# Recurrent gates of a hybrid decoder layer: a block's high and low halves stacked on the contraction

## The chip, the cores and the metric

The kernel runs on one core of one Trainium2 chip. The metric is the device time of one execution in microseconds (us). The core has a matrix engine (TensorE, PE in the profile), a vector engine (VectorE, DVE), an activation engine (ScalarE, ACT), GpSimd (POOL) and a queue that issues transfers (SyncE, SP). Each engine takes its instructions strictly in the order of its own queue; they meet only through semaphores.

## The reference, cut to what matters

One decoder layer on 512 tokens of width 1024, in fp32. A combined projection gives the inputs of a recurrent branch (`u_x`, `u_g`), of an attention branch (`q`, `k`, `v`) and two branch gates. The part that is changed is the two gates of the recurrent branch; each is a block-diagonal product with 16 blocks of 64 x 64:

```python
xb = x.reshape(B, S, LRU_BLOCKS, LRU_BLOCK_W)             # 16 blocks of 64
r = sigmoid(einsum('bsnc,ncd->bsnd', xb, w_r).reshape(B, S, W) + b_r)
i = sigmoid(einsum('bsnc,ncd->bsnd', xb, w_i).reshape(B, S, W) + b_i)
log_a = -LRU_C * r * softplus(-lam)
a = exp(log_a);  u = sqrt(-expm1(2 * log_a)) * (i * x)
h = scan of h[t] = a[t] * h[t-1] + u[t]
y_lru = h * gelu(u_g)
```

Then follow stick-breaking attention on 16 heads of 64, the merge of both branches, an MLP of width 4096 and a gated embedding.

## The kernel before

**Precision.** TensorE takes fp32r operands. A helper `split` (lines 54 to 56) makes of each fp32 operand a high part (a cast on ScalarE, L55) and a low part (the rest, a subtraction on VectorE, L56). A product is then three matmuls (`prod`, L122 to L124): high by high, high by low, low by high. A projection of 128 output channels has eight contraction tiles, so 24 matmuls of 128x512.

**Stages.** The value projections come first, until about 53 us. Then, in the pool `lru` (line 283), eight projections `ux` with the convolution (`conv`: a copy out of PSUM on ScalarE, L316, one activation, L317, three VectorE steps, L319), and eight projections `ug`, whose PSUM is copied by L379. Between them stand the gate products (`gate_products`, line 322) of 128 channels each, that is, of two blocks, on the diagonal of one 128x128 stationary tile that is zero elsewhere. Four 128-channel groups make a half, which `lru_mid` (line 338) turns into the recurrence: exp, tanh, square and a square root on ScalarE (L345 to L349, each on 128x2048), products and scans on VectorE (L348 to L354); a gelu (L385) and a product (L386) end it. After that the attention pools open: for each of eight pairs of heads a query and a key projection (`ps_q`, `ps_k`), their splitting (`qk_evac`: casts L410, L412, L413 on ScalarE, subtractions L411, L414 on VectorE), scores `z` (L423, L424) and so on. The merge, the MLP and the end follow.

**What sets the order.** The source is one sequence; a scheduler orders each engine's queue from it, using a timeline that it works out while the kernel is built. So a change in one place can shift the order of a queue far behind it. Three things matter beside data dependencies: PSUM tiles turn in rings (three of `pp` for the projections, three of `pg` for the gate products); the split weights (`whi`, `wlo`) turn in rings of three, so the cast of a projection's weights waits until the projection three places earlier is done; and the attention's tiles use the memory of the pool `lru`, so the first cast of `qk_evac` waits for the last use of that pool, the product L386 of the second half.

Of the kernel before, what the change touches and what calls it, by code (L numbers as in the profile page):

```python
# [8 lines left out]
F32 = mybir.dt.float32  # L9
F32R = mybir.dt.float32r  # L10
I32 = mybir.dt.int32
AF = mybir.ActivationFunctionType
ALU = mybir.AluOpType
PSUM = bass.MemoryType.PSUM

P = 128
S = 512
D = 1024
KT = D // P
# [3 lines left out]
DH = 64  # L23
# [11 lines left out]
def hybrid_layer(ctx, tc, xT, pT, vecs, gfin, gates, w_in, w_bl, w_ba, w_out,  # L35
# [9 lines left out]
    def f32(ap):  # L45
        return ap.bitcast(F32)


    def load_raw(src, name):
        raw = wp.tile([P, 1024], F32, tag="raw", name="raw_" + name)  # L50
        sy.dma_start(raw, src)
        return raw

    def split(hi, lo, src):
        sc.copy(hi, src)  # L55
        ve.tensor_tensor(lo, src, f32(hi), op=ALU.subtract)  # L56
# [62 lines left out]
    def prod(ps, pairs, first=True, last=True):  # L119
        n = len(pairs)  # L120
        for i, (lh, ll, rh, rl) in enumerate(pairs):
            pe.matmul(ps, lh, rh, start=(first and i == 0), stop=False)  # L122
            pe.matmul(ps, lh, rl, start=False, stop=False)  # L123
            pe.matmul(ps, ll, rh, start=False, stop=(last and i == n - 1))  # L124
# [12 lines left out]
    def vec(name, k):  # L137
        return vt[:, VECS.index(name), k:k + 1]
# [144 lines left out]
    with tc.tile_pool(name="lru", bufs=1) as lp, \  # L283
# [17 lines left out]
        ve.tensor_scalar(nl, nl, 0.0, 8.0, op0=ALU.max, op1=ALU.mult)  # L301
        ve.scalar_tensor_tensor(sp8, acc, 16.0, nl, op0=ALU.mult, op1=ALU.add)

        rawg = load_raw(gates, "gates").rearrange("p (g k n) -> p (g k) n", g=2, k=8)
        gh = lp.tile([P, 2 * KT, P], F32R, name="gh")
        gl = lp.tile([P, 2 * KT, P], F32R, name="gl")
        gp.memset(f32(gh), 0.0)
        gp.memset(f32(gl), 0.0)
        for j in range(2):
            q = slice(j * DH, (j + 1) * DH)  # L310
            split(gh[q, :, j * DH:(j + 1) * DH], gl[q, :, j * DH:(j + 1) * DH], rawg[q, :, :])

        def conv(ps, n, c):
            up = lp.tile([P, S + 4], F32, tag="up", name=f"up{n}", bufs=2)
# [6 lines left out]

        def gate_products(n, c, r, i):
            cs = lp.tile([P, 2, S], F32R, tag="cs", name=f"cs{n}", bufs=2)
            split(cs[:, 0, :], cs[:, 1, :], c)
            for g, (dst, b) in enumerate(((r, "br"), (i, "bi"))):
                ps = pgp.tile([P, S], F32, tag="pg", name=f"pg{g}_{n}")
                t = g * KT + n
                prod(ps, [(gh[:, t, :], gl[:, t, :], cs[:, 0, :], cs[:, 1, :])])
                sc.activation(dst, ps, AF.Sigmoid, bias=vec(b, n))

        groups = []

# [27 lines left out]
        for n in range(KT):  # L360
# [3 lines left out]
            cl, r, i = groups[-1]  # L364
# [541 lines left out]
```

## Time and profile before

| | |
|---|---|
| median of 3 runs | 928.24 us (928.11 to 929.11) |
| the profiled execution | 929.34 us, its span 927.6 us |
| TensorE busy | 914.0 us, 99% of the span |
| VectorE, ScalarE, GpSimd busy | 620.7, 505.8 and 67.5 us |
| granted TensorE clock, mean | 0.995 |

TensorE is busy nearly all of the span. A matmul of 128x512 lasts 0.39 us in the records, but they start 0.23 us apart, since they are pipelined; the start-to-start step is what a matmul costs. In the same way ScalarE's and VectorE's records overlap a little when nothing is waited for. Times below are counted from the span's start. The profile's last section lists waits that were inferred from semaphore events.

### The profile page before, as it was taken

How to read it: one execution, taken by the hardware profiler on the slowest of the kernel's cores; microseconds unless marked ns; L12 is line 12 of the kernel's file. 1: busy time of each engine (PE TensorE's matmuls, PEld its weight loads, DVE VectorE, ACT ScalarE, POOL GpSimd, SP SyncE). 2: the span in 40 equal slices, each digit the busy share in tenths (PEclk: the TensorE clock that was granted, in tenths of full speed). 3: DMA queues.
4: the chain of work that ended last, by engine and by line, in shares of the span. 5: the costliest groups of instructions: out<-in, count | busy, mean ns of one | idle time of the engine just before them, and what ended most of it. 6: DMA issues, size and time to landing. Idle time of an engine off the chain costs nothing. (4 is left out here: it accounts for less than half of the span.)

```text
span 927.6 us, 12721 instructions
## 1 busy us (share of the span) xinstructions
PE 914.0 (99%) x4858; PEld 790.3 (85%) x4858; DVE 620.7 (67%) x891; ACT 505.8 (55%) x802; POOL 67.5 (7%) x147
## 2 busy tenths in 40 slices
PE   9989999999999999999999999999999999999996
PEld 7878888888888888888888999999988888888885
DVE  6698665988998896433547878878853443443646
ACT  6355869667776765512325566777663332342523
POOL 0010000133233332000000000000000000000000
PEclk9999999999999999999999999999999999999998
DMA  6332232322222221342222233333333332443002
GB/s 240 102 114 69 69 113 69 114 70 69 69 69 69 69 69 53 131 157 90 91 91 92 91 92 114 93 113 101 112 130 113 115 114 94 152 140 114 1 1 91
DMA packets 25116, 89.46 MB, mean 96 GB/s; under 512 B 2912, under 2 KB 2912, under 8 KB 24800
## 3 DMA queue, kind: packets, MB, share of 16 engines
q1 hardware_dynamic: 24480, 87.61, 29.1%
q10 hardware_dynamic: 576, 1.05, 0.3%
q8 instruction: 38, 0.62, 0.3%
q14 instruction: 22, 0.18, 0.1%
HBM read 86.55 MB, written 2.10 MB: 96 GB/s over the span
## 5 line engine op out<-in xcount | busy, mean ns | idle before, releaser
L123 PE MATMUL dn<-wlo_dn,ring 128*128 128x512 f32 x256 | 99.6, 390 | 0.0
L124 PE MATMUL dn<-whi_dn,ring 128*128 128x512 f32 x256 | 99.5, 389 | 0.0
L122 PE MATMUL dn<-whi_dn,ring 128*128 128x512 f32 x256 | 97.4, 390 | 0.2 <-ACT whi_dn L55 0.2
L56 DVE TENSOR_TENSOR ring<-act,ring 128x512 fp32r<-128x512 f32 x32 | 22.0, 691 | 79.8 <-ACT ring L55 79.8
L55 ACT CAST ring<-act 128x512 fp32r<-128x512 f32 x32 | 19.6, 623 | 97.1 <-PE dn L123 97.1
L432 DVE TENSOR_TENSOR_SCAN pr<-r,zero 128x128 f32<-128x128 f32 (+1 forms) x64 | 54.1, 846 | 10.6 <-POOL r L160 10.1
L122 PEld LDWEIGHTS dn<-whi_dn,ring 128*128 128x128 f32 x256 | 48.0, 188 | 10.5 <-ACT whi_dn L55 0.5
L123 PEld LDWEIGHTS dn<-wlo_dn,ring 128*128 128x128 f32 x256 | 48.1, 188 | 10.0
L124 PEld LDWEIGHTS dn<-whi_dn,ring 128*128 128x128 f32 x256 | 48.1, 188 | 9.8
L56 DVE TENSOR_TENSOR wlo_dn<-raw_dn,whi_dn 128x1024 fp32r<-128x1024 f32 x32 | 39.2, 1226 | 22.7 <-ACT whi_dn L55 22.7
L428 ACT ACTIVATE r<-z 128x128 f32<-128x128 f32 (+1 forms) x64 | 28.5, 445 | 27.7 <-PE z L424 27.0
L160 POOL TENSOR_SCALAR_AFFINE_SELECT r<-r 128x128 f32<-128x128 f32 x64 | 29.8, 466 | 179.5 <-ACT r L428 175.0
L55 ACT CAST whi_up<-raw_up 128x1024 fp32r<-128x1024 f32 x24 | 25.1, 1047 | 30.1 <-PE upX L623 11.4
L56 DVE TENSOR_TENSOR wlo_up<-tw,whi_up 128x1024 fp32r<-128x1024 f32 x28 | 34.2, 1224 | 4.8 <-ACT whi_up L55 4.8
L55 ACT CAST whi_up<-tw 128x1024 fp32r<-128x1024 f32 x28 | 29.3, 1046 | 14.8 <-PE upZ L623 8.1
L621 PE MATMUL upA<-xa,whi_up 128*128 128x256 f32 x128 | 36.3, 284 | 0.0
L624 PE MATMUL upY<-xa,wlo_up 128*128 128x256 f32 x128 | 36.3, 283 | 0.0
L623 PE MATMUL upY<-xa,whi_up 128*128 128x256 f32 x128 | 36.3, 283 | 0.0
L624 PE MATMUL upA<-xa,wlo_up 128*128 128x256 f32 x128 | 36.3, 283 | 0.0
L623 PE MATMUL upA<-xa,whi_up 128*128 128x256 f32 x128 | 36.3, 283 | 0.0
L621 PE MATMUL upY<-xa,whi_up 128*128 128x256 f32 x128 | 36.3, 283 | 0.0
L55 ACT CAST whi_dn<-raw_dn 128x1024 fp32r<-128x1024 f32 x32 | 33.5, 1046 | 4.9 <-PE dn L124 4.1
(334 smaller groups left out, 2859.7 us busy)
## 6 DMA issues: line engine op xcount, KB each, us to landing
raw_up<-in_w_up_dram SPq DMA_DIRECT2D x32, 512.0 KB, 3.9
raw_dn<-in_w_dn_dram SPq DMA_DIRECT2D x32, 512.0 KB, 3.2
raw_u<-in_w_in_dram SPq DMA_DIRECT2D x16, 512.0 KB, 3.3
raw_qk<-in_w_in_dram SPq DMA_DIRECT2D x16, 512.0 KB, 3.4
raw_gl<-in_w_in_dram SPq DMA_DIRECT2D x8, 512.0 KB, 3.4
raw_ga<-in_w_in_dram SPq DMA_DIRECT2D x8, 512.0 KB, 3.4
raw_bl<-in_w_bl_dram SPq DMA_DIRECT2D x8, 512.0 KB, 3.4
raw_ba<-in_w_ba_dram SPq DMA_DIRECT2D x8, 512.0 KB, 3.4
```

The costliest lines, as they stand in the source:

```text
L55: sc.copy(hi, src)
L56: ve.tensor_tensor(lo, src, f32(hi), op=ALU.subtract)
L122: pe.matmul(ps, lh, rh, start=(first and i == 0), stop=False)
L123: pe.matmul(ps, lh, rl, start=False, stop=False)
L124: pe.matmul(ps, ll, rh, start=False, stop=(last and i == n - 1))
L160: gp.affine_select(block, block, pattern=[[-1, P]], compare_op=ALU.is_gt, fill=fill, base=0, channel_multiplier=1)
L428: sc.activation(r[:, 0:w], z[:, 0:w], AF.Sigmoid, scale=-0.125)
L432: ve.tensor_tensor_scan(pr[:, 0:w][:, ::-1], r[:, 0:w][:, ::-1], zero.broadcast_to([P, w]), 1.0, op0=ALU.mult, op1=ALU.add)
L621: pe.matmul(o, wh[:, k, c], x[:, 0, k, :], start=(first and fi == 0 and k == 0), stop=False, skip_group_check=True)
L623: pe.matmul(o, wh[:, k, c], x[:, 1, k, :], start=False, stop=False, skip_group_check=True)
L624: pe.matmul(o, wl[:, k, c], x[:, 0, k, :], start=False, stop=(k == 3), skip_group_check=True)
```

## The change

A gate block of 64 channels has a contraction of only 64 rows. Before, two blocks share a stationary tile (block-diagonal, half of it zero), and each of the two gates needs three matmuls for the pair: six for 128 channels. In the change, `cs` holds one block in each of its two halves: the block's high part on its own 64 partitions, its low part on the other 64. The stationary tile `gh` holds the high weights of both gates side by side (2 x 64 columns), twice: on the upper and on the lower 64 partitions. One matmul then gives high by high plus high by low, for both gates. `gl` holds the low weights on the block's own partitions and zeros on the others, and a second matmul adds low by high. That is two matmuls for a block, four for 128 channels.

The two gates of a block come out in the two halves of one PSUM tile, so the sigmoids run on 64 partitions each: four for 128 channels where there were two. `cs` is made by two casts and two subtractions of 64x512 where there was one of each of 128x512; the subtraction writes to the other 64 partitions. While the weights are prepared, four casts and four subtractions of 64x512 take the place of two and two of 64x1024, two copies of 64x1024 (the second copy of `gh`) are added, and the memset of `gh` goes.

```diff
--- before.py
+++ after.py
@@ -301,14 +301,19 @@
         ve.tensor_scalar(nl, nl, 0.0, 8.0, op0=ALU.max, op1=ALU.mult)
         ve.scalar_tensor_tensor(sp8, acc, 16.0, nl, op0=ALU.mult, op1=ALU.add)
 
-        rawg = load_raw(gates, "gates").rearrange("p (g k n) -> p (g k) n", g=2, k=8)
-        gh = lp.tile([P, 2 * KT, P], F32R, name="gh")
-        gl = lp.tile([P, 2 * KT, P], F32R, name="gl")
-        gp.memset(f32(gh), 0.0)
+
+
+        rawg = load_raw(gates, "gates").rearrange("p (g k n) -> p k g n", g=2, k=8)
+        gh = lp.tile([P, KT, 2, P], F32R, name="gh")
+        gl = lp.tile([P, KT, 2, P], F32R, name="gl")
         gp.memset(f32(gl), 0.0)
         for j in range(2):
             q = slice(j * DH, (j + 1) * DH)
-            split(gh[q, :, j * DH:(j + 1) * DH], gl[q, :, j * DH:(j + 1) * DH], rawg[q, :, :])
+            o = slice((1 - j) * DH, (2 - j) * DH)
+            for g in range(2):
+                c = slice((g ^ j) * DH, ((g ^ j) + 1) * DH)
+                split(gh[q, :, j, c], gl[q, :, j, c], rawg[q, :, g, :])
+            sc.copy(gh[o, :, j, :], f32(gh[q, :, j, :]))
 
         def conv(ps, n, c):
             up = lp.tile([P, S + 4], F32, tag="up", name=f"up{n}", bufs=2)
@@ -321,12 +326,16 @@
 
         def gate_products(n, c, r, i):
             cs = lp.tile([P, 2, S], F32R, tag="cs", name=f"cs{n}", bufs=2)
-            split(cs[:, 0, :], cs[:, 1, :], c)
-            for g, (dst, b) in enumerate(((r, "br"), (i, "bi"))):
-                ps = pgp.tile([P, S], F32, tag="pg", name=f"pg{g}_{n}")
-                t = g * KT + n
-                prod(ps, [(gh[:, t, :], gl[:, t, :], cs[:, 0, :], cs[:, 1, :])])
-                sc.activation(dst, ps, AF.Sigmoid, bias=vec(b, n))
+            for j in range(2):
+                q = slice(j * DH, (j + 1) * DH)
+                o = slice((1 - j) * DH, (2 - j) * DH)
+                sc.copy(cs[q, j, :], c[q, :])
+                ve.tensor_tensor(cs[o, j, :], c[q, :], f32(cs[q, j, :]), op=ALU.subtract)
+                ps = pgp.tile([P, S], F32, tag="pg", name=f"pg{j}_{n}")
+                pe.matmul(ps, gh[:, n, j, :], cs[:, j, :], start=True, stop=False)
+                pe.matmul(ps, gl[:, n, j, :], cs[:, j, :], start=False, stop=True)
+                sc.activation(r[q, :], ps[q, :], AF.Sigmoid, bias=vec("br", n)[q, :])
+                sc.activation(i[q, :], ps[o, :], AF.Sigmoid, bias=vec("bi", n)[q, :])
 
         groups = []
 
```

Three places of the built order. First TensorE's queue where the last channels' gate products (`pg_7`) stand, among the last two `ug` projections (`ps_ug_1193` before is the seventh of eight). Before:

```order
L122 MATMUL ps_ug_1193<-hT,whi_u_0_1164 128x512
L123 MATMUL ps_ug_1193<-hT,whi_u_0_1164 128x512
L122 MATMUL pg_7_1020<-cs_1017,gh 128x512
L123 MATMUL pg_7_1020<-cs_1017,gh 128x512
L124 MATMUL pg_7_1020<-cs_1017,gl 128x512
L122 MATMUL pg_7_1025<-cs_1017,gh 128x512
L123 MATMUL pg_7_1025<-cs_1017,gh 128x512
L124 MATMUL pg_7_1025<-cs_1017,gl 128x512
L124 MATMUL ps_ug_1193<-hT,wlo_u_0_1165 128x512
```

And of the change, where `ps_ug_1246` is the eighth projection and six of its matmuls stand ahead of the first row:

```order
L122 MATMUL ps_ug_1246<-hT,whi_u_1_1217 128x512
L123 MATMUL ps_ug_1246<-hT,whi_u_1_1217 128x512
L335 MATMUL pg_7_1039<-cs_1036,gh 128x512
L336 MATMUL pg_7_1039<-cs_1036,gl 128x512
L124 MATMUL ps_ug_1246<-hT,wlo_u_1_1218 128x512
L335 MATMUL pg_7_1046<-cs_1036,gh 128x512
L336 MATMUL pg_7_1046<-cs_1036,gl 128x512
```

The last gate products moved from the seventh projection, behind its 2nd matmul, into the eighth, behind its 8th. In the change the seventh projection (`ps_ug_1214`) has six gate matmuls among its 24, those of channels 5 and 6. The second place is ScalarE's queue from the last gates to the square root of the second half. Before:

```order
L329 ACTIVATE r_786<-pg_7_1020,vt 128x512
L329 ACTIVATE i_787<-pg_7_1025,vt 128x512
L345 ACT_TABLE_LOAD
L345 ACTIVATE a_1257<-r_786 128x2048
L346 ACTIVATE r_786<-r_786 128x2048
L347 ACTIVATE t_1258<-a_1257 128x2048
L55 CAST whi_qk_1_1307<-raw_qk_1_1305 128x1024
L379 COPY y_lru<-ps_ug_1193 128x512
L349 ACT_TABLE_LOAD
L349 ACTIVATE r_786<-r_786 128x2048
```

Of the change, which continues three rows later with `qk_evac`'s first cast (between them the weight casts `whi_gl_0` and `whi_gl_1`):

```order
L338 ACTIVATE i_798<-pg_7_1046,vt 64x512
L354 ACT_TABLE_LOAD
L354 ACTIVATE a_1278<-r_797 128x2048
L55 CAST whi_qk_0_1359<-raw_qk_0_1357 128x1024
L388 COPY y_lru<-ps_ug_1246 128x512
L355 ACTIVATE r_797<-r_797 128x2048
L356 ACTIVATE t_1279<-a_1278 128x2048
L394 ACT_TABLE_LOAD
L394 ACTIVATE y_lru<-y_lru 128x2048
L55 CAST whi_qk_1_1551<-raw_qk_1_1549 128x1024
L358 ACT_TABLE_LOAD
L358 ACTIVATE r_797<-r_797 128x2048
```

The gelu with its table load and a weight cast (`whi_qk_1`) moved ahead of the square root; before, they stand behind it. The third place is VectorE's queue from the product with the square root to the subtraction that the first scores need (`qs`). Before:

```order
L352 TENSOR_TENSOR r_786<-r_786,i_787 128x2048
L56 TENSOR_TENSOR wlo_qk_0_1339<-raw_qk_0_1336,whi_qk_0_1338 128x1024
L354 SCALAR_TENSOR_TENSOR i_787<-a_1257,r_786 128x512 x4
L56 TENSOR_TENSOR wlo_qk_1_1531<-raw_qk_1_1528,whi_qk_1_1530 128x1024
L386 TENSOR_TENSOR y_lru<-i_787,y_lru 128x2048
L56 TENSOR_TENSOR wlo_gl_0_1562<-raw_gl_0_1559,whi_gl_0_1561 128x1024
L411 TENSOR_TENSOR qs_1366<-ps_q_1304,qs_1366 64x512
```

Of the change:

```order
L361 TENSOR_TENSOR r_797<-r_797,i_798 128x2048
L56 TENSOR_TENSOR wlo_gl_0_1583<-raw_gl_0_1580,whi_gl_0_1582 128x1024
L363 SCALAR_TENSOR_TENSOR i_798<-a_1278,r_797 128x512 x4
L395 TENSOR_TENSOR y_lru<-i_798,y_lru 128x2048
L56 TENSOR_TENSOR wlo_gl_1_1813<-raw_gl_1_1810,whi_gl_1_1812 128x1024
L420 TENSOR_TENSOR qs_1387<-ps_q_1325,qs_1387 64x512
L423 TENSOR_TENSOR kl<-ps_k_1356,kh_1388 64x512
L420 TENSOR_TENSOR qs_1610<-ps_q_1548,qs_1610 64x512
L420 TENSOR_TENSOR qs_1387<-ps_q_1325,qs_1387 64x512
```

The chain of products and scans is the same; one weight subtraction fewer stands inside it, and another pair's `qs_1610` comes before the second `qs_1387`. TensorE's order around the first scores has not moved: in both kernels the four score matmuls `z` stand directly behind the second pair's query projection, and that pair's key projection directly behind them.

## Rows read from the trace of the kernel before

**Rows 1.** Page of the profile: busy time, share of the span, instructions of each engine

```profile
PE 914.0 (99%) x4858; PEld 790.3 (85%) x4858; DVE 620.7 (67%) x891; ACT 505.8 (55%) x802; POOL 67.5 (7%) x147
```

**Rows 2.** Windows: busy time by engine, granted clock (PEclk), around the first projections

```profile
52.00:58.00 6.00, 3.46 (x15) 2.52 (x14) 6.00 (x17) 4.76 (x6) 3.63 (x4) 0.97 0.25 89
58.00:64.00 6.00, 6.00 (x22) 4.83 (x21) 5.70 (x17) 1.86 (x3) 0.00 (x0) 0.75 0.32 96
56.10:165.00 108.90, 108.90 (x470) 89.50 (x471) 79.03 (x117) 77.77 (x87) 1.81 (x9) 0.98 0.27 90
```

**Rows 3.** Waits of TensorE, whole span: in total us, times, longest us

```profile
PE ps_ux L122 <- DVE vs L230: 2.5, 1, 2.5
PE wt L167 <- POOL onesf L154: 1.2, 1, 1.2
PE pv L122 <- ACT whi_v L55: 0.7, 1, 0.7
PE dn L122 <- ACT whi_dn L55: 0.2, 1, 0.2
```

**Rows 4.** The gate products' PSUM tile: count, duration ns min/median/max, first and last start

```profile
L122 PE MATMUL pg<-cs,gh x16: 392/397/398, 73.2 to 145.2; 128*128 128x512 f32 x16
...
L329 ACT ACTIVATE r<-pg,vt x8: 688/688/691, 74.8 to 145.5; 128x512 f32<-128x512 f32 x8
```

**Rows 5.** Timeline of TensorE: start us, duration us, instruction

```profile
68.70 0.39 PE L122 MATMUL ps_ux<-hT,whi_u 128*128 128x512 f32 x1
...
144.07 0.39 PE L122 MATMUL ps_ug<-hT,whi_u 128*128 128x512 f32 x1
...
172.71 0.39 PE L423 MATMUL z<-kh,qs 128*128 128x128 f32 x2
...
173.17 0.43 PE L122 MATMUL ps_k<-hT,whi_qk 128*128 128x512 f32 x1
```

**Rows 6.** ScalarE by line and shape, 60 to 150 us: one conv activation

```profile
L317 ACT ACTIVATE c<-up,vt 128x512 f32<-128x512 f32 x8 | 6.5, 815 | 0.2
```

**Rows 7.** Timeline of ScalarE from the last gates to the first attention cast

```profile
140.97 1.84 ACT L329 ACTIVATE i<-pg,vt 128x512 f32<-128x512 f32 x3
142.70 0.59 ACT L379 COPY y_lru<-ps_ug 128x512 f32<-128x512 f32 x1
...
145.47 0.69 ACT L329 ACTIVATE r<-pg,vt 128x512 f32<-128x512 f32 x1
...
148.11 1.92 ACT L345 ACTIVATE a<-r 128x2048 f32<-128x2048 f32 x1
...
153.69 1.03 ACT L55 CAST whi_qk<-raw_qk 128x1024 fp32r<-128x1024 f32 x1
...
155.22 1.28 ACT L349 ACT_TABLE_LOAD   x1
156.52 1.92 ACT L349 ACTIVATE r<-r 128x2048 f32<-128x2048 f32 x1
...
159.87 1.28 ACT L385 ACT_TABLE_LOAD   x1
...
162.99 1.03 ACT L55 CAST whi_qk<-raw_qk 128x1024 fp32r<-128x1024 f32 x1
...
169.79 0.58 ACT L410 CAST qs<-ps_q 64x512 fp32r<-64x512 f32 x1 [1.49 <-DVE y_lru L386]
```

**Rows 8.** Timeline of VectorE at the same hand-over

```profile
158.47 2.29 DVE L352 TENSOR_TENSOR r<-r,i 128x2048 f32<-128x2048 f32 x1 [1.22 <-ACT r L349]
...
167.41 2.28 DVE L386 TENSOR_TENSOR y_lru<-i,y_lru 128x2048 f32<-128x2048 f32 x1
169.62 1.22 DVE L56 TENSOR_TENSOR wlo_gl<-raw_gl,whi_gl 128x1024 fp32r<-128x1024 f32 x1
170.86 0.68 DVE L411 TENSOR_TENSOR qs<-ps_q,qs 64x512 fp32r<-64x512 f32 x1
...
172.29 0.69 DVE L411 TENSOR_TENSOR qs<-ps_q,qs 64x512 fp32r<-64x512 f32 x1
```

## The prediction

> **What bounds the kernel now.** I read the page's first lines, then the windows by stage, the waits of TensorE, the gate products' tile, and last the timelines of three engines where the recurrent stage hands over to attention. The page says what sets the time: TensorE is busy 99% of the span [rows 1]. The waits say it more sharply: after its wait of 2.5 us ahead of the first `ux` projection TensorE waits for no other engine until a 0.2 us wait far behind, in the MLP [rows 3]. So from 56.1 us on, a matmul less is time gained, and a stall is time lost, each in full. The reader is to see next that the other engines keep up with some room but not with much: from 56.1 to 165 us ScalarE works 77.8 and VectorE 79.0 of 108.9 us [rows 2]. At one place there is hardly any room. The second pair's query projection ends and the first scores start at 172.71 [rows 5]; they need `qs`, whose first subtraction ran from 170.86 to 171.54, and the key projection behind them, at 173.17, takes over a PSUM tile that the second subtraction released at 172.98 [rows 5, 8], 0.2 us before. That chain starts where the first cast of `qs` waits for the last recurrent product, L386 [rows 7].
>
> **What it takes from TensorE.** Six gate matmuls for 128 channels become four, 48 become 32 (16 of each of three kinds before, one of which is in [rows 4]). They do not cost their 0.39 us but the step between starts. From the third `ux` projection's first matmul, 68.70, to the seventh `ug` projection's, 144.07 [rows 5], lie 12 projections of 24 and 42 gate matmuls, 330 steps in 75.37 us, 0.2284 us each. Sixteen fewer are 3.65 us. By that alone TensorE would reach the first scores at 172.71 - 3.65 = 169.06.
>
> **What it gives the others.** ScalarE: 16 sigmoids more. A sigmoid of 64 partitions is not in the trace; the nearest rows say that partitions do not matter, since a cast of 64x512 takes 0.58 and a copy of 128x512 0.59 [rows 7], so I take the step of a full one, (142.70 - 140.97) / 3 = 0.577 us [rows 7], and half of it as the other end. That is 9.2 us (4.6 at the other end). Eight casts of 64x512 more at 0.58 are 4.6 us. Preparing the weights adds two copies of 64x1024, 1.03 each by the 128x1024 cast [rows 7], and splits two casts into four, 0.2 us; together 16.1 us (11.5). VectorE: eight subtractions at 0.68 [rows 8], 5.4 us, and some 0.3 us for the weights. That they write to the other 64 partitions costs nothing extra: the `qs` subtractions do the same. GpSimd loses a memset, half of its 3.6 us in the window from 52 to 58 [rows 2]; nothing waits for it on TensorE.
>
> Does the block loop carry this? Per 128 channels TensorE now needs 28 x 0.2284 = 6.4 us. ScalarE needs a weight cast and a copy, 1.53 us from 153.69 to 155.22 [rows 7], the convolution's activation, 0.82 [rows 6], two casts, 1.16, and four sigmoids, 2.31: 5.8 us. So it does, and I cost the loop, the weight preparation (a weight half is due only at 68.70, some 11 us later) and the early groups at nothing. The cover is 0.6 us for each group; once `lru_mid` puts its big functions on top, ScalarE falls behind TensorE, and the lost time shows at the end of the stage.
>
> The Trainium skill has a rule that speaks against the change: TensorEngine Tiling (Array Packing), section PSUM Bottleneck, says that packing the array speeds up TensorE but not the emptying of PSUM, which can then become the limit. By the page the evacuating engine sets the stage; by the rows above it does not in the loop, 5.8 against 6.4, and what it would cost is the third rival.
>
> **The hand-over, worked out.** In the change's order the last gate products stand in the eighth `ug` projection. From 68.70 on, 288 projection and 22 gate matmuls come before the seventh, so it starts at 68.70 + 310 x 0.2284 = 139.50; its 24, six gate matmuls and eight more of the eighth make 38, so the two of the first block start at 148.18 and 148.41. Before, the third matmul of `pg_7`'s first tile stood four steps behind 144.07, at 144.98, and its sigmoid began at 145.47 [rows 5, 7], 0.49 later; now it begins at 148.90. ScalarE isn't late there: it has to wait for the seventh projection to end, at 146.4, for a weight cast, so its earlier backlog is made up.
>
> From there ScalarE's queue, in the order that stands in the section on the change: four sigmoids 2.31; table load 1.28; exp, tanh and square 5.58 (148.11 to 153.69); weight cast and copy 1.53; table load and gelu 3.12 (159.87 to 162.99); weight cast 1.03; table load and square root 3.22 (155.22 to 158.44) [rows 7]. Sum 18.07: 166.97. Then VectorE's product, weight subtraction, scans and last product, which took from 158.47 to 169.69, 11.22 us with two weight subtractions [rows 8], now have one, 1.22 less: 10.0 us, so that the last product ends at 177.0, 7.3 us later than before. Then a weight subtraction with its step of 1.24 (169.62 to 170.86), and four subtractions (`qs`, `kl`, the other pair's `qs`, the second `qs`) with steps of 0.715 (half of 170.86 to 172.29) [rows 8], the last taking 0.69: 181.05. ScalarE's casts beside them (five at 0.58 from 177.1) end at 180.0, so they fit. The key projection follows 0.2 later, at 181.25. TensorE came to the scores at 169.06 and has nothing else in its queue; it stands still for about 9.4 us until the scores, and for over two more between them and the key projection. So at the key projection the change is 181.25 - 173.17 = 8.1 us behind, the 3.65 us already counted.
>
> **The clock.** The only long gap before was the 2.5 us [rows 3]; behind it the granted clock fell from 1.00 to a mean of 0.97 over one 6 us window and 0.75 over the next [rows 2], the lower level of 1.2 GHz for some 3.4 us, and that cost 0.03 x 6 + 0.25 x 6 = 1.7 us of full-speed work. A gap four times as long at the scores should bring at least that back: 1.7 us, with 0 (matmuls waiting for attention anyway) and twice as much, 3.4, as ends. The Trainium skill says in TensorE: Matmul & The Clock Gate, section Why this matters for your kernels, that gaps between bursts of matmuls bring the half clock back. By that rule the gap costs the clock too and the sum is the one below; without it the sum is 1.7 us less; the row after the 2.5 us gap agrees with the rule.
>
> **Sum.** 8.1 + 1.7 = 9.8 us later from the second pair's key projection on. What follows is TensorE's own work, the same number of matmuls, and nothing there waited [rows 3], so the end shifts by as much: a span of 927.6 + 9.8 = 937.4, an execution of 929.34 + 9.8 = 939.1. The profiled execution lies 1.1 us above the median of the runs, 928.24; I predict from the median: 938.0 us.
>
> **Rivals.** First, the stall as worked out, 0.70. Its own range: the sigmoids at half the price take 1.2 us off this chain, a backlog or a table load out of step adds 2 us, the clock 0 to 3.4: 934 to 942.
>
> Second, the other side, 0.09: the gain arrives. The condition is one point: the last recurrent product would have to end by 177.0 - (181.25 - 169.5) = 165.2, so that the key projection finds its tile at 169.5. Then only the 16 matmuls count and the time is 928.24 - 3.65 = 924.6. For it speaks that ScalarE and VectorE have 31 and 30 us of idle time in the stage [rows 2] and the added work is 16.1 and 5.7; against it that the idle time lies before the last gates, while the chain of 18.1 + 10.0 us behind them has none, and the last gates cannot come before TensorE's 148.4.
>
> Third, ScalarE as the bound of the whole stage, 0.10: TensorE would wait for `cs`, for sigmoids that free the ring of three, or for weight casts, group by group, because every one of ScalarE's waits stays and its work comes on top: up to 16.1 us instead of the one stall, 944.3, and 941 to 946 where attention's new order adds small stalls to the first case. Against it speak 5.8 against 6.4 us for a group and VectorE's and ScalarE's room.
>
> Fourth, the stall shrinks to the gain, 0.04: TensorE stands still for 2 to 5 us only, no clock is lost, 926.5 to 930. The chain behind the last gates, 28 us, would have to be shorter by some 8. The remaining 0.07 is a smaller stall of the same kind, 930 to 934.
>
> The range holds the first case and most of its neighbours: 931.5 to 943. Of the chances for faster or slower by 0.2% (1.9 us, about what a measurement of this kernel can tell from no change), the first, the third and the rest give slower 0.87, the fourth mostly no difference, 0.03, and the second, with a bit of the fourth, faster 0.10.
>
> **What would show it.** In the changed profile: 32 gate matmuls with starts 0.23 apart, and TensorE without a wait from 56 to about 169 us; the first `pg_7` sigmoid near 149 and the square root's end near 167; the first cast of `qs` near 177, waiting for the last product; one wait of TensorE of some 9 us at the first `z`, another of one to two us at `ps_k`, both laid to VectorE's `qs`; a window behind them with a clock below 1.00. It is wrong where TensorE waits for `cs`, `pg` or `whi` in the loop (third rival), or has no wait at `z` (second), or where attention shows waits of its own.

## The result and the profile after

The changed kernel takes 938.09 us (median of 5 runs, 937.47 to 940.35) where the kernel before takes 928.24 (927.98 to 929.35): a ratio of 1.0107, 95% interval 1.0094 to 1.0119. The prediction was 938.0 us, range 931.5 to 943.0, with a chance of 0.87 for slower. The profiled execution took 940.35 us, its span 938.6.

The first lines, as in [rows 1 to 3]: the page's busy times, the windows by stage (us; busy us and count of TensorE, weight loads, VectorE, ScalarE, GpSimd; granted clock; DMA share; GB/s) and TensorE's waits (total us, times, longest).

```profile
PE 912.9 (97%) x4842; PEld 786.9 (84%) x4842; DVE 626.9 (67%) x901; ACT 523.8 (56%) x830; POOL 63.5 (7%) x146
```

```profile
56.10:165.00 108.90, 108.77 (x471) 89.64 (x472) 81.21 (x124) 94.00 (x112) 0.80 (x6) 0.98 0.27 90
178.00:184.00 6.00, 3.79 (x10) 2.94 (x11) 4.49 (x7) 5.85 (x12) 0.54 (x2) 0.50 0.26 90
184.00:190.00 6.00, 6.00 (x24) 4.87 (x23) 2.07 (x6) 1.47 (x5) 0.86 (x3) 0.75 0.00 0
```

```profile
PE z L432 <- DVE qs L420: 10.4, 1, 10.4
...
PE ps_k L122 <- DVE qs L420: 0.7, 1, 0.7
```

From 56.1 to 165 us ScalarE now works 94.0 us instead of 77.8, and TensorE still never waits there. The whole loss stands in two new rows, `z` and `ps_k`, and in a granted clock of 0.50 and 0.75 in the two windows from 178 to 190 us. The same windows in the kernel before:

```profile
178.00:184.00 6.00, 6.00 (x30) 4.99 (x29) 5.58 (x9) 5.22 (x9) 2.08 (x4) 1.00 0.27 98
184.00:190.00 6.00, 6.00 (x32) 5.03 (x31) 4.65 (x8) 3.52 (x9) 1.40 (x4) 1.00 0.23 76
```

The gate products' tile, against [rows 4], and TensorE's timeline (start, duration, instruction), against [rows 5]:

```profile
L335 PE MATMUL pg<-cs,gh x16: 397/397/398, 74.3 to 148.7; 128*128 128x512 f32 x16
...
L337 ACT ACTIVATE r<-pg,vt x16: 668/684/688, 76.2 to 150.2; 64x512 f32<-64x512 f32 x16
```

```profile
147.99 0.40 PE L335 MATMUL pg<-cs,gh 128*128 128x512 f32 x1
...
168.66 0.39 PE L124 MATMUL ps_q<-hT,wlo_qk 128*128 128x512 f32 x1
179.48 0.77 PE L432 MATMUL z<-kh,qs 128*128 128x128 f32 x2 [10.43 <-DVE qs L420]
...
181.63 0.77 PE L122 MATMUL ps_k<-hT,whi_qk 128*128 128x512 f32 x1 [0.74 <-DVE qs L420]
...
186.89 0.44 PE L122 MATMUL ps_k<-hT,whi_qk 128*128 128x512 f32 x1
```

Sixteen of each matmul in place of sixteen of three; a sigmoid of 64 partitions lasts 684 ns, as long as one of 128 (688). TensorE is done with the second query projection at 168.66 + 0.23 = 168.9 instead of 172.7, stands still for 10.43 us, and then takes its key projection in steps of 0.43 us (the lower of the clock's levels, 1.2 GHz) until 186.89.

ScalarE from the first group's exp on, past the second group's first gates, and VectorE at the hand-over, against [rows 7, 8]:

```profile
105.69 1.92 ACT L354 ACTIVATE a<-r 128x2048 f32<-128x2048 f32 x1
...
128.62 2.10 ACT L337 ACTIVATE r<-pg,vt 64x512 f32<-64x512 f32 x3 [2.82 <-DVE i L363]
...
148.76 0.68 ACT L337 ACTIVATE r<-pg,vt 64x512 f32<-64x512 f32 x1
149.45 0.69 ACT L338 ACTIVATE i<-pg,vt 64x512 f32<-64x512 f32 x1
...
165.30 1.92 ACT L358 ACTIVATE r<-r 128x2048 f32<-128x2048 f32 x1
...
177.59 0.58 ACT L419 CAST qs<-ps_q 64x512 fp32r<-64x512 f32 x1 [7.69 <-DVE y_lru L395]
```

```profile
167.25 2.29 DVE L361 TENSOR_TENSOR r<-r,i 128x2048 f32<-128x2048 f32 x1 [2.00 <-ACT r L358]
...
175.19 2.29 DVE L395 TENSOR_TENSOR y_lru<-i,y_lru 128x2048 f32<-128x2048 f32 x1
```

The reader is to follow one chain: last gates 148.76, square root 165.30, product with it 167.25, last recurrent product 175.19, and the cast of `qs` at 177.59 that had waited for it for 7.69 us.

### The profile page after: what moved, and what is told of

It is laid out like the page before. It is cut to its first block, busy times and chain, and to the rows that moved or that the text cites. A ratio compares the mean times of both kernels' runs of the same rounds, so it can differ in the third digit from the quotient of the medians.

```text
span 938.6 us, 12736 instructions
## 1 busy us (share of the span) xinstructions
PE 912.9 (97%) x4842; PEld 786.9 (84%) x4842; DVE 626.9 (67%) x901; ACT 523.8 (56%) x830; POOL 63.5 (7%) x146
## 5 line engine op out<-in xcount | busy, mean ns | idle before, releaser
L56 DVE TENSOR_TENSOR ring<-act,ring 128x512 fp32r<-128x512 f32 x32 | 21.9, 691 | 79.8 <-ACT ring L55 79.8
```

## The experiments

Twelve kernels were run beside the kernel before. All times below are medians; the ratio is to the kernel before on the same chip, where it took between 928.5 and 929.5 us. One per cent is 9.3 us; the change itself is 1.0107. The number ahead of a run is that of the experiment below, and the edits there are cut to the lines that matter.

| run | us | ratio [95%] | expected by theory, us or ratio |
|---|---|---|---|
| 6: r and i in two buffers | 929.23 | 1.0005 [0.9996, 1.0013] | 924.6 |
| 6: before with the same | 929.90 | 1.0006 [0.9998, 1.0015] | 928.2 |
| 1: full sigmoids | 924.84 | 0.9964 [0.9952, 0.9976] | 925.1 |
| 4: gap filled | 937.75 | 1.0096 [1.0081, 1.0111] | 935.5 |
| 3: gelu last | 936.96 | 1.0082 [1.0069, 1.0095] | 935.1 |
| 2: before, sigmoids cut | 934.80 | 1.0065 [1.0053, 1.0077] | 930.4 |
| 5: qs, kh in own memory | 934.28 | 1.0055 [1.0043, 1.0068] | 927 |
| 7: two buffers, copies on VectorE | 930.54 | 1.0017 [1.0008, 1.0025] | 925.5 |
| 8: mixed tile, 8 buffers | 935.20 | 1.0066 [1.0053, 1.0080] | 0.9963 |
| 9: mixed tile, 4 buffers | 935.84 | 1.0079 [1.0065, 1.0093] | 0.997 to 1.001 |
| 10: mixed tile, i in two buffers | 929.68 | 1.0006 [0.9997, 1.0015] | 0.997 |
| 11: first group only | 927.33 | 0.9983 [0.9974, 0.9992] | 0.998 |

**1. Full sigmoids: is it the cut sigmoids?**

```diff
-    sc.activation(r[q, :], ps[q, :], AF.Sigmoid, bias=vec("br", n)[q, :])
-    sc.activation(i[q, :], ps[o, :], AF.Sigmoid, bias=vec("bi", n)[q, :])
+    dst, b = ((r, "br"), (i, "bi"))[j]
+    sc.activation(dst, ps, AF.Sigmoid, bias=vec(b, n))
```

> The changed kernel with one sigmoid of 128 partitions for each PSUM tile in place of two of 64: r is taken from the first tile and i from the second, so the gates are mixed up among the channels; matmuls, casts and subtractions are those of the change. In its order the last gates stand in the seventh ug projection and the gelu behind the square root, as before. Theory (the sigmoids cut in two make ScalarE late): last gates 141.8, first sigmoid near 142.3 instead of 145.47 before, so the chain of 27.7 from there to the second pair's key projection ends at 170.0 against TensorE's 169.5: 925.1 (924.6 to 926.5). Rival D (the stacking itself, casts in two pieces and subtractions that cross partitions, makes the chain late): half of the loss or more stays, 933 or more.

Measured 0.9964, 3.3 us faster than before: nearly the 3.65 us of the sixteen matmuls (a wait of 0.3 us at `ps_k` is left). With the change at 1.0107, sixteen sigmoids more or less, with the order that the scheduler builds for each, decide over 13.3 us. Rival D is out: stacked matmuls, cut casts and subtractions across partitions are all still in this kernel. ScalarE's timeline in it:

```profile
98.73 1.93 ACT L354 ACTIVATE a<-r 128x2048 f32<-128x2048 f32 x1
...
121.62 1.27 ACT L338 ACTIVATE r<-pg,vt 128x512 f32<-128x512 f32 x2 [1.49 <-DVE i L363]
...
141.66 0.69 ACT L338 ACTIVATE r<-pg,vt 128x512 f32<-128x512 f32 x1
...
166.03 0.58 ACT L419 CAST qs<-ps_q 64x512 fp32r<-64x512 f32 x1 [2.21 <-DVE y_lru L395]
```

The first group's exp starts at 98.73, in the changed kernel at 105.69. The second group's first sigmoids start at 121.62 against 128.62, each time when the first group's scans give `r` free; last gates at 141.66 against 148.76; the first `qs` cast at 166.03 against 177.59. So the seven microseconds were lost early, in the `ux` projections, and handed on by `r` and `i`, which have one buffer. How much of them is the sigmoids' own time and how much the order of the queues that came with them, this run doesn't tell; experiment 11 has a figure for it.

**2. The kernel before with cut sigmoids: is the cut enough by itself?**

```diff
-    sc.activation(dst, ps, AF.Sigmoid, bias=vec(b, n))
+    for q in (slice(0, DH), slice(DH, P)):
+        sc.activation(dst[q, :], ps[q, :], AF.Sigmoid, bias=vec(b, n)[q, :])
```

> The kernel before with each gate sigmoid cut into two of 64 partitions, 16 more, and nothing else of the change: 48 gate matmuls as before. Theory (the cut sigmoids lengthen the chain at the hand-over): last gates' matmuls some 0.7 us later in the seventh ug projection, four sigmoids of 0.70 for two of 0.6, 1.6 us: the key projection waits about 2.1 us, with up to 0.5 for the clock: 928.2 + 2.2 = 930.4 (929.3 to 932). Rival G (the sigmoids' extra time lies in ScalarE's idle time, and the late gates come from the matmuls' new order): 928.2.

Slower by 0.65%, 6.0 us, where 2.2 were expected: the direction is the theory's (rival G is out), the size is not. TensorE's waits and ScalarE's timeline in this kernel:

```profile
PE z L424 <- DVE qs L412: 2.6, 1, 2.6
...
PE ps_k L122 <- DVE qs L412: 0.3, 1, 0.3
...
PE z L425 <- DVE kl L415: 0.2, 1, 0.2
```

```profile
142.36 4.20 ACT L330 ACTIVATE i<-pg,vt 64x512 f32<-64x512 f32 x6
...
148.62 1.38 ACT L330 ACTIVATE r<-pg,vt 64x512 f32<-64x512 f32 x2
```

Six cut sigmoids of `i` take 4.20 us where three whole ones took 1.84 [rows 7], and the last gates' first sigmoid starts at 148.62, 3.15 later than before. The waits sum to 3.1 us; the granted clock of 0.72 from 178 to 184 us is another 1.7. The profiled execution also comes to the first `ux` projection 1.3 us later than before (57.42 for 56.10), ahead of any cut sigmoid; what sets that isn't shown, the other profiled executions have it between 55.57 and 57.38, and 1.3 of the 3.15 us are this late start. The expectation had counted the four sigmoids of the last gates only. That is the term it missed: here the cut sigmoids further ahead cost time at the hand-over too.

**3. Gelu last: does the order on ScalarE matter?**

```diff
+    with tc.issue_after(root[g].ins):     # root[g]: the group's square root
         sc.activation(yg, yg, AF.Gelu_apprx_tanh)
```

> The changed kernel with each group's gelu ordered behind that group's square root on ScalarE, as it stood before; nothing else moves. Theory (the wait at the first scores is the length of the chain behind the last gates): the square root starts at 162.2, when VectorE's product L357 is done, and not at 165.3; the last recurrent product ends at 174.5 in place of 177.5; TensorE's wait at z shrinks from 10.4 to 7.4: 938.1 - 3.0 = 935.1 (934.3 to 936). Rival F (the wait is set by something else than this chain, such as weight casts or the score tiles): 938.1.

```profile
PE z L434 <- DVE qs L422: 7.3, 1, 7.3
```

The wait is 7.3 us, as the theory has it, and 2.3 us are won (1.0082 against 1.0107; 3.0 expected). The last product starts at 172.31 instead of 175.19. So the wait at `z` is the length of this chain, and rival F is out; the gelu's place in the order accounts for about a quarter of the loss.

**4. The gap filled with matmuls: what does the clock cost?**

```diff
     z = pz.tile([P, S], F32, tag="z", name=f"z{p}_{j}_{qb}")
+    if (p, j, qb) == (0, 0, 0):
+        with tc.issue_after(state["last"].ins):   # the second query projection's end
+            for k in range(46):
+                pe.matmul(z, hT[:, 0, k % KT, 0:P], hT[:, 1, k % KT, :], start=True, stop=True)
```

> The changed kernel with 46 extra matmuls into the first score tile between the second pair's query projection and the first scores (46 x 0.228 = 10.5 us, the length of the gap); the real scores overwrite them. The second query projection is written one step earlier in the program; the order on the engines around it is otherwise that of the change. Theory (the half clock behind the gap is the gap's doing): clock 1.00 up to and behind the scores, key projection from its start at full rate, 13 steps of 0.43 become 0.228, 2.6 us won: 935.5 (935.0 to 936.5). Rival E (the clock falls for another reason, or matmuls at half rate only wait for attention's tiles anyway): 938.1.

The time doesn't decide: 1.0096 against 1.0107, 1.0 us, with intervals that overlap. TensorE's timeline and two windows of this kernel say more:

```profile
168.42 10.59 PE L435 MATMUL z<-hT 128*128 128x512 f32 x46
...
181.16 0.47 PE L122 MATMUL ps_k<-hT,whi_qk 128*128 128x512 f32 x1 [0.92 <-DVE qs L420]
...
181.93 0.60 PE L122 MATMUL ps_k<-hT,whi_qk 128*128 128x512 f32 x1
...
185.31 0.42 PE L124 MATMUL ps_k<-hT,wlo_qk 128*128 128x512 f32 x1
```

```profile
178.00:184.00 6.00, 4.76 (x17) 3.40 (x16) 4.57 (x8) 5.85 (x12) 0.62 (x3) 0.83 0.24 87
184.00:190.00 6.00, 6.00 (x27) 4.88 (x26) 2.64 (x6) 2.07 (x5) 1.95 (x5) 0.89 0.00 0
```

The filler runs for 10.59 us without a gap, up to the scores, but the key projection falls to steps of 0.43 us at 181.93 all the same, for some eight steps instead of twelve; clock 0.83 and 0.89 instead of 0.50 and 0.75. What TensorE did before the fall was four short matmuls with a wait of 0.33 us among them, a wait of 0.92 us and three matmuls at full rate. So the long gap answers for a part of the clock's price. The thin stretch at its end is left as the likely cause of the rest, which no run here fills. The Trainium skill (TensorE: Matmul & The Clock Gate, section Why this matters for your kernels) lays the half clock to idle gaps between bursts; this trace agrees on the direction, and adds that filling the one long gap isn't enough.

**5. `qs` and `kh` in memory of their own: is the wait the reuse of memory?**

```diff
+    qkp = apart.enter_context(tc.tile_pool(name="qkp", bufs=2, side="right"))
-    qs = ap.tile([P, 2, S], F32R, tag="qs", name=f"qs{p}")
+    qs = qkp.tile([P, 2, S], F32R, tag="qs", name=f"qs{p}")      # kh likewise
```

> The changed kernel with attention's qs and kh in memory of their own, and no longer in what the recurrent stage's tiles leave; kl and the rest stay there. Theory (TensorE waits because the first cast of qs waits for the last recurrent product, whose tiles it takes over): qs is cast and subtracted beside the chain; TensorE waits some 1.5 us at z, for kh behind ScalarE's square root, and some 0.5 at the key projection, which starts near 171.6 in place of 181.6; the lower scores come later, behind other projections: 928.2 - 3.65 + 2.1 + up to 1 for the clock = 927 (925.5 to 930). Rival H (attention needs ScalarE and VectorE at that time, whichever memory it has): the scores' functions and scans come late and TensorE waits for them further on, 934 to 938.

```profile
PE ps_gl L122 <- DVE qs L422: 2.2, 1, 2.2
PE z L434 <- ACT kh L424: 1.4, 1, 1.4
...
PE ps_k L122 <- DVE qs L422: 1.0, 1, 1.0
```

Half right. The key projection starts at 172.55, nine microseconds earlier, as expected. But VectorE's queue then holds the next subtraction of `qs` behind the last recurrent product, and the `gl` projection waits 2.2 us for the PSUM tile that it frees. Waits of 4.6 us, and a clock of 0.72, 0.90 and 0.81 in the three windows from 172 to 190, leave 1.0055. Reused memory is the route by which the chain reaches TensorE, but with that route closed the in-order queue is the next; both theories had a share.

**6. `r` and `i` in two buffers: does it help to let the second group start early?**

```diff
-    r = lp.tile([P, GN, S], F32, tag="r", name=f"r{g}")
+    r = lp.tile([P, GN, S], F32, tag="r", name=f"r{g}", bufs=2)  # i likewise
```

> The changed kernel with r and i in two buffers each, so that the second group's gates need not wait for the first group's scans and last product. In its order the last gates stand in the fifth ug projection and not in the eighth. Theory (all of the loss is the late hand-over to attention): the last recurrent product ends near 161, before TensorE comes to the first scores at 169.06; no wait at z, clock at full speed behind, and only the 16 matmuls count: 928.2 - 3.65 = 924.6 (924.2 to 925.5). Rival A (ScalarE's and VectorE's added work costs of its own, wherever it lies): the work is all still there, 932 or more. Rival B (what is lost lies in the gate matmuls or in attention itself): 938.

> The kernel before with r and i in two buffers each: the control for the run above. Theory: TensorE lost nothing at the hand-over before, so nothing is to be won, 928.2 (927.7 to 928.6). Rival C (two buffers are worth something by themselves, and the changed kernel's gain with them is theirs): 920 to 925.

The control is 1.0006: two buffers are worth nothing to the kernel before, and rival C is out. The changed kernel goes from 1.0107 to 1.0005, which returns the loss but not the gain. Its window and TensorE's waits:

```profile
110.00:160.00 50.00, 47.49 (x207) 38.20 (x207) 34.67 (x34) 49.34 (x53) 0.00 (x0) 1.00 0.21 74
```

```profile
PE pg L335 <- DVE cs L333: 1.4, 1, 1.4
...
PE ps_ug L124 <- DVE wlo_u L56: 1.0, 1, 1.0
...
PE z L432 <- ACT kh L422: 0.2, 1, 0.2
```

The hand-over is nearly mended (0.2 us at `z`), but ScalarE is now busy 49.3 of 50 us, and TensorE waits for `cs` and for a weight half. TensorE's steps show what these waits cost: 118.45 to 119.86, 135.22 to 137.02 and 155.98 to 156.44, with one slower step behind each, are 3.3 us more than full rate, nearly all of the gain of 3.65. So rival A was right in part: the added work has a price of its own as soon as it can no longer lie in idle time. Whether the price is ScalarE's load isn't shown. The casts for the late `cs` ended on ScalarE at 134.05, and its subtractions started on VectorE at 136.19, behind the first group's scans (130.62 to 135.18).

**7. The same, with the copies of `ug` on VectorE.**

```diff
-    sc.copy(y_lru[:, n, :], ps)
+    ve.tensor_copy(y_lru[:, n, :], ps)
```

> The changed kernel with r and i in two buffers, as in the first run, and the eight copies of the ug projections out of PSUM done by VectorE in place of ScalarE. In the first run ScalarE was busy 49.3 of 50 us from 110 to 160 and TensorE waited 1.4 us for cs and 1.0 us for a weight half there. Theory (ScalarE's load in that stretch bounds the stage once the gates come early): 8 x 0.58 = 4.6 us less on ScalarE, those 2.4 us of waits go, the last product comes before TensorE reaches the scores: 925.5 (924.6 to 927). Rival J (those waits come from VectorE's queue, which now has eight copies more): 929 or more.

```profile
PE ps_ug L124 <- DVE wlo_u L56: 2.4, 2, 1.6
```

Missed: 1.0017, no faster than without (1.0005; the intervals overlap). The wait for `cs` is gone, that for VectorE's `wlo_u` has doubled, as rival J says, and one of 1.1 us at `ps_k` for VectorE's `qs` is new. The Trainium skill (TensorEngine Tiling (Array Packing), section PSUM Bottleneck) advises to empty PSUM with both ScalarE and VectorE; here that won nothing, and the wait that grew is for VectorE's queue, which also makes every weight's low part.

**8 to 10. One whole sigmoid into a tile of its own, sorted by VectorE.** With i's columns on the block's own partitions:

```diff
+    u = lp.tile([P, S], F32, tag="u", name=f"u{j}_{n}", bufs=8)   # 4, 5 in the next two
+    sc.activation(u, ps, AF.Sigmoid, bias=mb[:, j, n:n + 1])
+    ve.tensor_scalar(r[q, :], u[o, :], spx[o, n:n + 1], None, op0=ALU.mult)
+    ve.tensor_tensor(i[q, :], u[q, :], c[q, :], op=ALU.mult)
```

> The changed kernel with one sigmoid of 128 partitions for each PSUM tile, as in the third run, but with nothing mixed up: i's columns stand on the block's own partitions and r's on the other 64, the sigmoid goes to a tile of its own (eight buffers), and VectorE takes r (times its decay, into the other 64 partitions) and i (times c) out of it in pieces of 64. Theory (ScalarE's sixteen more sigmoids and the late gates are the loss, TensorE's 16 matmuls the gain): ScalarE as in the third run, VectorE 8 scalings of some 0.48 and 8 products of 0.69 more, 9.4 us, over 95 us in which it has 20 idle; gates in the fifth ug projection at the latest; no wait at the scores: 924.8 on a day when the kernel before takes 928.2 (ratio 0.9963, 0.995 to 0.998). Rival K (VectorE becomes the bound, since it also makes every weight's low part): waits for wlo or cs as in the last run, ratio 0.999 to 1.004.

> The same with four buffers for the sigmoid's tile, so that the second group's gates have to wait for the first group's scans and last product once more; in its order the last gates stand in the seventh ug projection and the second gelu ahead of the square root. Theory: last gates near 141.5; the chain behind them with the gelu inside, some 26 + 3 us less one sigmoid, ends near the time TensorE reaches the key projection, 169.5, or 1 to 2 us later: ratio 0.997 to 1.001. Rival K as above: VectorE's load, the same in both, gives the same time in both.

Both missed, by about 1%. The longest wait of the first and of the second:

```profile
PE ps_ug L124 <- DVE wlo_u L56: 4.2, 1, 4.2
```

```profile
PE z L438 <- DVE qs L426: 7.2, 1, 7.2
```

With eight buffers there is no wait at the scores any more: ScalarE is relieved, as expected. But VectorE's queue has eight products with `i` in a row, from 145.45 to 151.0, behind the first group's last product, and the weight half behind them comes 4.2 us late. With four buffers the wait is back at `z`. So in the first it looks like a tile with one buffer that blocks an in-order queue, and not like VectorE's load as such (rival K). The third tells these apart, with `i` in two buffers and five for the sigmoid's tile:

> The mixed tile with i in two buffers and five for the sigmoid's tile. In the last two runs the wait had moved: with eight buffers VectorE had eight products with i queued behind the first group's last product L401 (it ends at 145.4, since i has one buffer), the weight half behind them came 4.2 us late, and the ug and q projections behind it waited 2.0 us more. Here each product with i stands where its sigmoid is, and only the scalings of r wait for the scans. Theory: no wait of TensorE above 1 us between 56 us and the scores, the last gates in the fourth to fifth ug projection, no long wait at z; ratio 0.997 (0.995 to 0.999), under 1 for the first time with the reference's numbers. Rival K (VectorE's load as such, busy 43.6 of 46 us from 64 to 110, makes something late wherever it is queued): waits of 2 us or more in the ug projections, ratio 1.001 to 1.005.

```profile
PE pg L344 <- DVE cs L342: 1.5, 1, 1.5
```

1.0006: nine tenths of the loss with eight buffers return while VectorE's busy time on the page stays the same (636.7 and 637.0 us), which rules the load out as the cause of that 4.2 us; but 0.997 isn't reached. What is left in the waits is one of 1.5 us for `cs`, behind the scans in VectorE's queue. From the start before it to the projection's next one behind the gates, 132.80 to 136.02, TensorE loses 2.1 us to it, and it comes to the second key projection at 171.65 where 168.9 was to be had. Where the rest of the way to 0.997 went isn't traced.

**11. The change for the first four tiles only.** If the same edit costs nothing where ScalarE has idle time and much on the chain to attention, half of it should win.

```diff
+    if n >= NS:                       # NS = 4: the second group as before
+        split(cs[:, 0, :], cs[:, 1, :], c)
+        for g, (dst, b) in enumerate(((r, "br"), (i, "bi"))):
+            prod(ps, [(gh[:, n, g, :], gl[:, n, g, :], cs[:, 0, :], cs[:, 1, :])])
+            sc.activation(dst, ps, AF.Sigmoid, bias=vec(b, n))
+        return
```

> The change for the first four channel tiles only, whose gates stand in the ux projections; the last four keep three matmuls per product and one sigmoid of 128 partitions for each, as before. ScalarE's order around the second group, and the place of the last gates in TensorE's, are those of the kernel before. Theory (the same edit costs nothing where ScalarE has room and everything where the chain to attention starts): 8 matmuls fewer, 1.8 us; 8 sigmoids and 4 pieces of cast more on ScalarE between 66 and 110 us, where it has 13 us idle before the edit; they push the first group's functions back by some 2 us, which the idle time ahead of the last gates (2 to 3 us before) takes up; no wait at z: ratio 0.998 (0.997 to 1.000). Rival L (the first group's delay passes through r and i, which have one buffer, to the last gates and so to attention): up to 2.5 us of wait at z and as much again for the clock, ratio 1.001 to 1.004.

0.9983, interval 0.9974 to 0.9992: faster than both kernels, by 1.6 us where eight matmuls are 1.8. ScalarE's and TensorE's timelines in it:

```profile
100.69 1.93 ACT L367 ACTIVATE a<-r 128x2048 f32<-128x2048 f32 x1
...
123.68 1.27 ACT L340 ACTIVATE r<-pg,vt 128x512 f32<-128x512 f32 x2 [2.27 <-DVE i L376]
...
138.70 1.85 ACT L340 ACTIVATE i<-pg,vt 128x512 f32<-128x512 f32 x3
...
143.20 0.69 ACT L340 ACTIVATE r<-pg,vt 128x512 f32<-128x512 f32 x1
...
167.51 0.58 ACT L432 CAST qs<-ps_q 64x512 fp32r<-64x512 f32 x1 [1.49 <-DVE y_lru L408]
```

```profile
170.90 0.44 PE L122 MATMUL ps_k<-hT,whi_qk 128*128 128x512 f32 x1
```

In the kernel before, the second group's first sigmoid stands here on ScalarE's timeline:

```profile
119.73 0.69 ACT L329 ACTIVATE r<-pg,vt 128x512 f32<-128x512 f32 x1 [1.08 <-DVE i L354]
```

It is now 4 us later, but the three of `i` that follow start at 138.70, 2.3 us earlier than in [rows 7], because ScalarE's queue ahead of them goes by TensorE again: its weight cast waits 1.38 us for a `ug` projection (136.33, before 138.60 with 1.39 us). TensorE brings the projections sooner: 1.8 us by the eight matmuls, and 0.35 because this execution starts its first `ux` projection at 55.75 and not at 56.10. From there everything is 2.3 us early: the last gates (143.20 for 145.47), the first `qs` cast (167.51 for 169.79) and the key projection (170.90 for 173.17), and TensorE waits at neither `z` nor `ps_k`. Rival L is out.

This run also says more on the seven microseconds of experiment 1. Its first group has all the cut sigmoids of the change, and its exp starts at 100.69, 2.0 us later than with full ones and not 7.0. Of the other five, 4.6 go with the order of the queues: in the changed kernel ScalarE waits 1.88 us for the third tile's gate products, until 92.48, and a weight cast, a copy and two casts for the next tile (101.68 to 104.37) stand ahead of the first group's exp, where here the like stand behind it. Another 0.5 is the later first `ux` projection (56.23 for 55.75). So the cut sigmoids made the changed kernel late in part by their own steps and in part by the order that was built around them; no run holds the order and changes the sigmoids alone.

## Why the prediction was right, step by step

**TensorE's gain.** Sixteen matmuls at 0.2284 us, 3.65: right. The second query projection ends at 168.9 (169.06 predicted), and experiment 1 returns 3.3 us of it as time.

**The others' work.** ScalarE 16.1 us predicted, 523.8 - 505.8 = 18.0 on the page, of which 94.00 - 77.77 = 16.2 lie from 56.1 to 165 us; VectorE 5.7, and 6.2 on the page. So ScalarE's sum was 1.9 us short, and the price that was low is the sigmoid's: sigmoids are busy 21.9 us for 10.8 before, 11.1 more and not 9.2. A cut one has a step of 0.70 (148.76 to 149.45 and on) and not the 0.577 of whole ones in a row, so the four of the last gates took 2.8 and not 2.3 us.

**The loop costs nothing.** Right for TensorE, which has no wait from 56 to 169 us, and wrong for the second group: its first sigmoid starts 8.9 us later than before (128.62 for 119.73). The prediction said that ScalarE falls behind once the big functions come on top, but gave that no size: it took the place of the last gates from the order of the changed kernel and so had the lateness in its sum. It also held that ScalarE makes its backlog up before the last gates, in a wait for the seventh projection. There was no such wait: ScalarE works without one from 128.62 to 168.1 us. It came to the last gates at 148.76, 0.53 us after their second matmul's start at 148.23, where 0.49 was reckoned. That it was free just then is luck. Its sentence that the last gates "cannot come before TensorE's 148.4" was true of that order and not of the change: in experiment 1 their first sigmoid starts at 141.66, in the first group's version at 143.20.

**The hand-over.** Predicted and measured: last gates' matmuls 148.18 and 147.99, first sigmoid 148.90 and 148.76, end of the square root 166.97 and 167.22, end of the last product 177.0 and 177.48, key projection 181.25 and 181.63. Right within 0.5 us, with the wait shared out as 10.43 at `z` and 0.74 at `ps_k` instead of 9.4 and over two. The 9.4 was a slip: by the prediction's own chain the first subtraction ends at 177.0 + 1.24 + 0.69 = 178.9, 9.9 us after 169.06. The share at `ps_k` shrank because the four score matmuls ran at the lower clock, 1.41 us (179.48 to 180.89) for 0.46 before. Experiments 3 and 5 show that this chain sets the wait; 1 and 2 that the cut sigmoids make it late.

**The clock.** Mis-sized: 1.7 us predicted. The first twelve steps of the key projection take 5.26 us (181.63 to 186.89) in place of 2.74, 2.5 more, inside the range of 0 to 3.4. Experiment 4 shows the mechanism in part: less gap, less half clock.

**The sum.** At the key projection 8.5 us (8.1 predicted), with the clock 11.0, which is the difference of the two profiled spans, 938.6 - 927.6 = 11.0. The medians differ by 9.85, the predicted 9.8. The profiled execution of the changed kernel is 2.3 us above its median, and which term is smaller in the others isn't shown. The prediction's own figure for the profiled execution, 939.1, is 1.3 us short of the 940.35 measured, so that it hit the median within 0.1 us is luck.

**The rivals.** The second (the gain arrives) asked for a last product that ends by 165.2; it ended at 177.48. The fourth asked for 2 to 5 us of standing still; it was 11.2. The third (ScalarE bounds the stage) did not happen in the change: TensorE has no wait for `cs`, `pg` or `whi` there. Waits of its kind, 2.4 us for `cs` and a weight half, came in experiment 6. That the waits move from one place to the next, `z`, `cs`, `wlo_u`, `ps_gl`, is what the prediction did not look for.

## What to carry to other kernels

In this kernel work taken from the busiest engine and given to one with idle time paid where that idle time is, not on average: ask for each piece whether it stands ahead of a hand-over, and apply the edit only to the pieces that don't. A tile with one buffer hands an early lateness on to the next group, so look for the first instruction that starts later, not for the wait at which it comes out. And before a wait is removed, ask what stands behind it in the in-order queue: in five of these runs shorter waits came up in another place.

## What the runs showed of the hardware

Activations of 64 partitions cost ScalarE more than half of one of 128 here: the duration is the same (684 and 688 ns), and they follow each other in steps of 0.70 us, while whole ones in a row have 0.577 [rows 7]; six cut ones take 4.20 us, three whole ones 1.84. Cutting a sigmoid so costs 2 x 0.70 - 0.58 = 0.82 us, 13 us for sixteen.

Waits of one to two microseconds that stand close together bring the half clock too: in the kernel with `qs` in its own memory 1.4 and 1.0 us, with two short matmuls between them, are followed by a clock of 0.72. The single wait of 2.2 us that comes 9 us later in that kernel is followed, three matmuls on, by steps of 0.43 us too. Behind a single wait of 1.5 us, in the mixed tile with `i` in two buffers, the clock stays at 1.00, and so it does behind waits of 1.1 and 0.4 us, 1.5 us apart, with the copies on VectorE. Nor is the answer to one wait fixed: the 2.5 us ahead of the first `ux` projection, which every kernel here has, is followed by 0.97 and 0.75 before [rows 2], and by 1.00 in both windows with the copies on VectorE:

```profile
52.00:58.00 6.00, 3.45 (x15) 2.55 (x14) 6.00 (x16) 4.60 (x8) 1.88 (x3) 1.00 0.25 89
58.00:64.00 6.00, 6.00 (x28) 4.95 (x27) 5.80 (x17) 3.91 (x5) 0.00 (x0) 1.00 0.13 40
```

These are profiled executions of different kernels. Executions of one kernel differ in their mean granted clock as well: with the copies on VectorE, the three shortest, at 0.997, took 929.36 to 929.51 us, and the two longest, at 0.994, took 931.45 and 932.89. In which stage the clock was lower there isn't shown, since only profiled executions show it by stage.
